# Two-layer diffusion backbone on one core: out projection of the last layer by token tiles in sequence, three modulation groups moved a layer ahead, first up tiles in two halves of the tokens

## The chip, the cores and the metric

The kernel runs on one core of one Trainium2 chip. The metric is device microseconds (us) from start to end of the program; lower is better. Engines are called PE (matmul; PEld is its weight load), DVE (vector), ACT (scalar), POOL (GpSimd) and SP (whose queue issues most DMAs).

## The reference

Two post-norm layers over 256 latent and 256 context tokens, width 1024. What the change touches:

```python
for i in range(DEPTH):                                   # DEPTH = 2
    need_ctx = i < DEPTH - 1                             # the last layer needs the latent tokens alone
    mod = (s_lat @ ada_w[i] + ada_b[i])[:, None, :]      # 1024 -> 6 * 1024
    sh1, sc1, g1, sh2, sc2, g2 = jnp.split(mod, 6, -1)
    u = modulate(h, sh1, sc1)                            # layer_norm(h) * (1 + sc1) + sh1
    ...                                                  # u @ w_in, then four token mixers
    mix = merge_branches((y_hy, y_sw, y_rw, y_df), p_gt, w_branch[i], w_out[i])   # ends with acc @ w_o
    h = layer_norm(DN_ALPHA * h + g1 * mix, ln1_g[i], ln1_b[i])
    f = conv_ffn(modulate(h, sh2, sc2), ffn_w_up[i], ffn_conv_w[i], ffn_conv_b[i], ffn_w_down[i])
    h = layer_norm(DN_ALPHA * h + g2 * f, ln2_g[i], ln2_b[i])
    ...                                                  # the same for the context tokens if need_ctx
```

## The kernel before

The 512 tokens are four tiles of 128: 0 and 1 context, 2 and 3 latent. Layer 0 works on all four, layer 1 (the last) on tiles 2 and 3 after its mixers have used the context; there `N.t0` is 256, the first token that counts. Every weight comes from HBM as a tile `w` of 128x1024 numbers (512 KB, by SP's queue, three buffers), is cast by ACT to `whi` (L197) and its remainder is taken by DVE or POOL as `wlo` (L201). Activations are split in the same way (`uh`/`ul`, `ah`/`al`), and every product is three matmuls: hi by hi, hi by lo, lo by hi. All matmuls of `mm` stand in one line (L174), all transposes in another (L178).

The work is written as Python generators that are woven by hand. `weave` runs a dense generator (matmuls of a projection) and, for a share of its cost, pulls steps from `N.work` (norms and the like). `col_tile` makes one 128-column tile of a projection: weight, then 24 matmuls over 8 values of k. It also pulls `N.rate` steps of the side generator `N.side`. The Tile framework's scheduler then orders each engine's instructions once more, so what stands next to what is only seen in the built program.

**Modulation.** `ada(l, groups)` makes the six modulation vectors of layer l in 12 groups. A group is 5 steps: four weight chunks (DMA `w<-in_adaw`, 512 KB each; matmuls `bkd<-w,sst`), then an ACT copy `adas`, four transposes `bkd<-cstt,adas` and a DVE reduction `mod`. Before, layer 1's groups 0 to 3 run beside the up tiles of layer 0's FFN, 4 to 9 beside the column tiles of layer 1's mixers (what is left over runs after the last of them, `N.weave(N.side, 0.0)`), and 10 and 11 after layer 1's out projection. `gate_out` and `gate_in` send a finished gate vector through HBM, to be broadcast.

**Out projection of the last layer** (`out_proj`, tiles 2 and 3, 8 weights k of `wout`, 96 matmuls of 512 columns). With `skew` 5, both tiles take k = 0 to 2; then tile 2 takes k = 3 to 7 while the weights are kept (three of them in tiles of their own, `wh`/`wl`), and tile 3 takes them after. The banks of tile 2 and the first half of tile 3 are called `bkd`, the last one `bko`. `finish` multiplies the banks by the gate and adds the residual, with sums. `hooks` issues the row vectors `lg`, `lb` and then loads and splits the first four weights of the FFN's up projection ahead (`pw`, to `ph`/`pl`).

**Tail.** For each tile: `sum_stats` (ACT square, POOL power), `post_norm` (two DVE operations), `sum_stats` again, `norm` to `xn` (one POOL operation of 1024 columns), `modulate` (8 transposes; for each k an ACT operation to `uh`, POOL to `u`, DVE to `ul`). Then the up tiles: 44 column tiles of 256 tokens.

Of the kernel before, what the change touches and what calls it, by code (L numbers as in the profile page):

```python
# [10 lines left out]
AF = mybir.ActivationFunctionType  # L11
ALU = mybir.AluOpType
# [100 lines left out]
class Feed:  # L113


    def __init__(self, net, items):
        self.net, self.items, self.loaded, self.ready = net, list(items), [], []
        self.cutting = iter(())
# [37 lines left out]
class Net:  # L156
    def __init__(self, ctx, tc, a, out):
        self.ctx, self.tc, self.nc, self.a, self.out = ctx, tc, tc.nc, a, out
        self.work, self.pre, self.pool_cols = [], [], 0
        self.side, self.rate = iter(()), 0  # L160
        self.lo = self.nc.vector
        self.aside, self.done, self.feed = [], set(), None
        self.ps = ctx.enter_context(tc.tile_pool(name="ps", bufs=1, space=PSUM))
        self.cp = ctx.enter_context(tc.tile_pool(name="cp", bufs=1))
        self.wp = ctx.enter_context(tc.tile_pool(name="wp", bufs=1))
        self.up = ctx.enter_context(tc.tile_pool(name="up", bufs=1))
# [76 lines left out]
    def dense(self, ps, hi, lo, c0, xh, xl, nk, t0, t1):  # L243

        for k in range(nk):
# [8 lines left out]
                self.feed.step()  # L254
            yield 3 * 0.216 * (t1 - t0) / 512

    def col_tile(self, src, part):

        hi, lo = self.wsplit(src)
        for _ in range(self.rate):  # L260
            next(self.side, None)
        ps = self.bank("d")[:, 0:part[1] - part[0]]
        yield from self.dense(ps, hi, lo, lambda k: k * 128, self.uh, self.ul, 8, *part)
        return ps
# [181 lines left out]
    def norm(self, src, dst, stats, pool=None):  # L446

        nc = self.nc
        m, rs = stats
        if pool is None:  # L450
            nc.vector.tensor_scalar(dst, src, m, rs, op0=ALU.subtract, op1=ALU.mult)
            return
        nm = pool.tile([128, 1], F32, tag="lnns", name="lnns", bufs=2)
        nc.vector.tensor_scalar(nm, m, rs, -1.0, op0=ALU.mult, op1=ALU.mult)
        nc.gpsimd.tensor_scalar(dst, src, rs, nm, op0=ALU.mult, op1=ALU.add)

    def u_tiles(self):
# [1174 lines left out]
    def out_proj(self, l, pool, src, nk, lhs, tiles, h, gate, tail, skew, hooks, folded):  # L1632

        nc = self.nc
        hooks = iter(hooks)

        def weight(k, last):
            w = self.wload(src(k))  # L1640
            if last and folded:
                g = gate[tiles[-2] // 2]
                c = 512
                nc.gpsimd.tensor_tensor(w[:, 0:c], w[:, 0:c], g[:, 0:c], ALU.mult)  # L1644
                nc.vector.tensor_tensor(w[:, c:1024], w[:, c:1024], g[:, c:1024], ALU.mult)
            x = k - nk + skew
            hl = None
            if last and 0 <= x < skew - 2:
                hl = [pool.tile([128, 1024], F32R, name=f"w{y}{x}") for y in "hl"]
            return next(self.wcut(w, 1, hl))  # L1650

        def step(w, i, k, halves=(0, 1)):
            (whi, wlo), (ah, al), ts = w, lhs(k), slice(i * 128 - self.t0, i * 128 + 128 - self.t0)
            for hf in halves:
                cs = slice(hf * 512, hf * 512 + 512)
                self.mm(ps[i, hf], ah[:, ts], whi[:, cs], k == 0, False)
                self.mm(ps[i, hf], ah[:, ts], wlo[:, cs], False, False)
                self.mm(ps[i, hf], al[:, ts], whi[:, cs], False, k == nk - 1)

        def finish(i):  # L1660
            sums = []
            for hf in range(2):
                sl = slice(hf * 512, hf * 512 + 512)
                if not folded:
                    nc.vector.tensor_tensor(ps[i, hf], ps[i, hf], gate[i // 2][:, sl], ALU.mult)
                sm = pool.tile([128, 1], F32, tag=f"lns{hf}", name="lns", bufs=2)
                nc.vector.scalar_tensor_tensor(h[i][:, sl], h[i][:, sl], ALPHA, ps[i, hf], ALU.mult, ALU.add, accum_out=sm)
                sums.append(sm)
            return sums
        pre = []  # L1670
        for p0 in range(0, len(tiles), 2):
            pr = tiles[p0:p0 + 2]
            last = p0 == len(tiles) - 2
            sk = skew if last else 0
            ps = {(i, hf): self.bank("m" if not last else "o" if i % 2 and hf else "d") for i in pr for hf in range(2)}
            ws = []
            for k in range(nk):
                w = pre.pop(0) if pre else weight(k, last)
                next(hooks, None)
                if k < nk - sk:  # L1680
                    for i in pr:
                        step(w, i, k)
                    yield 2.6
                else:
                    ws.append(w)
                    step(w, pr[0], k)
                    yield 1.3
            if not last:
                pre = [weight(k, p0 == len(tiles) - 4) for k in range(2)]
                self.pool_cols = 320  # L1690
            if not last:
                self.work.append(tail([(i, finish(i)) for i in pr]))
                continue
            self.work.append(tail([(pr[0], finish(pr[0]))]))
            for hf in range(2):
                for x in range(sk):
                    step(ws[x], pr[1], nk - sk + x, [hf])
                    yield 0.65
            self.work.append(tail([(pr[1], finish(pr[1]))]))
        for _ in hooks:  # L1700
            pass
# [38 lines left out]
def backbone(ctx, tc, a, out):  # L1740
    N = Net(ctx, tc, a, out)
    nc = tc.nc
# [4 lines left out]
    for l in range(DEPTH):  # L1747
        need_ctx = l == 0
# [1 line left out]
        streams = (0, 1) if need_ctx else (1,)  # L1750
        N.t0 = 0 if need_ctx else 256
        n = 512 - N.t0
        N.side = N.ada(l, range(4 if l else 4, 10))
        ox = ExitStack()
        if 1:
            with ExitStack() as mx:
# [110 lines left out]
                with ExitStack() as ax:  # L1867
# [5 lines left out]
                    N.weave(N.swa_cols(l, ap_, need_ctx, xs), 0.0)  # L1873
                    N.weave(N.side, 0.0)
                    N.gate_out(l, 16, 0.5)
                    N.rate = 0
                    dp_ = ax.enter_context(tc.tile_pool(name="dp", bufs=1))
                    N.feed = Feed(N, [(a["win"][l, T_DF + t], None) for t in DF_ORDER]
# [46 lines left out]
        op = ox.enter_context(tc.tile_pool(name="op", bufs=1, side="right"))  # L1925
        lg, lb = (op.tile([128, 1024], F32, name=x) for x in ("lg", "lb"))
        N.u_tiles()
        kc, npre = (3, 4) if need_ctx else (0, 4)
        fx, fwx = ExitStack(), ExitStack()
        if kc:  # L1930
            fp1 = fx.enter_context(tc.tile_pool(name="fp1", bufs=1))
# [2 lines left out]
        def hooks():  # L1934
            yield
            G = [lambda t=t, x=x: nc.sync.dma_start(t, a[x][l].partition_broadcast(128))
                 for t, x in ((lg, "ln1_g"), (lb, "ln1_b"))]
            W = [lambda x=x: N.ahead(fw, a["wup"][l, x]) for x in range(npre)]
            for f in W + G if l == 0 else G + W:
                f()  # L1940
                yield

        def tail(its):
            xs = []
            for i, sums in its:
# [6 lines left out]
            yield from N.modulate(op, l, 1, xs, its[0][0])  # L1952
        N.pool_cols = 0 if need_ctx else 0
        N.weave(N.out_proj(l, op, lambda k: a["wout"][l, k], 8, lambda k: ahl[k], tiles, N.h, g1, tail,
                           (2 if need_ctx else 5), hooks(), l == 1 and 0), 0.4)
        hid = []

        def more2(k, part):
# [3 lines left out]
        if kc:  # L1962
            N.pre = (N.pre + [None] * (2 * kc - npre)) * 2
            N.side, N.rate = N.ada(0, (10, 11)), 2
            with tc.tile_pool(name="fu", bufs=1) as fu:
                N.weave(N.ffn_up(l, fu, [(k, CTX) for k in range(kc)], 256, hid, fp1, more2), 0.5)
                N.weave(N.side, 0.0)
                N.gate_out(l, 40, 1.0)
                N.flush()
                N.pool_cols = 0  # L1970
                ox.close()
                N.weave(N.ffn_up(l, fu, [(k, LAT) for k in range(kc)], 256, hid, fp1, more2), 0.0)
            fwx.close()
        else:
            N.weave(N.ada(l, (10, 11)), 0.0)
            N.gate_out(l, 40, 1.0)
            N.flush()
            N.pool_cols = 0
            ox.close()
        if 1:  # L1980
            fp2 = fx.enter_context(tc.tile_pool(name="fp2", bufs=1))
            with tc.tile_pool(name="fu", bufs=1) as fu:
                fdx = ExitStack()
                fd = fdx.enter_context(tc.tile_pool(name="fd", bufs=1, side="right"))
                g2 = {s: fd.tile([128, 1024], F32, name=f"g2{s}") for s in streams}
                lg, lb = N.row_vec(fd, "ln2_g", l, "lg"), N.row_vec(fd, "ln2_b", l, "lb")
                if l == 0:
                    N.side = N.ada(1, range(4))
                N.weave(N.ffn_up(l, fu, [(k, (N.t0, 512)) for k in range(kc, NKD)], n, hid, fp2,
                                 more2), 0.1)  # L1990
                N.weave(N.side, 0.0)
                N.rate = 0
                N.flush()
# [107 lines left out]
```

## Time and profile before

| | |
|---|---|
| three runs | 1866.68, 1867.2, 1871.5 us; median 1867.2 us |
| profiled execution | 1865.73 us, of which the span from the first to the last instruction is 1863.7 us |
| mean granted clock of TensorE | 0.967 |
| busy share of the span | PE 91%, PEld 72%, DVE 62%, ACT 42%, POOL 34% |
| chain that ended last | PE 60%, DVE 15%, ACT 5%, POOL 3%, DMA 3% |
| DMA | 241.37 MB, mean 130 GB/s |

PE is busy nine tenths of the span, but not evenly: for long stretches every microsecond is full, and in a few (the end of the last layer's out projection is one) it waits for norms. A matmul that is added costs its whole time in the first kind, and nothing in the second.

### The profile page before, as it was taken

Reading aid. Unit: us, or ns where it says so; the run is one execution under the profiler, and the core shown is the slowest. Engines: PE = TensorE matmul, PEld = TensorE weight load, DVE = VectorE, ACT = ScalarE, POOL = GpSimd, SP = SyncE. Lnnn points to the kernel's source line nnn. Section 1 sums busy time; section 2 is a strip of 40 time slices with the busy share of each in tenths; the row PEclk is TensorE's granted clock in tenths of the full one; section 3 lists DMA queues with packets and bytes.
Section 4 is the critical chain, followed back from the end, with each engine's and each line's share of the span. In section 5 each row is a group of like instructions: output and inputs, shape, how many; then the busy total and the mean of one; then the engine's idle time right before and its main releaser. Section 6 shows DMA issues by size and latency. Waiting matters only on the chain.

```text
span 1863.7 us, 36355 instructions
## 1 busy us (share of the span) xinstructions
PE 1704.9 (91%) x14618; PEld 1347.3 (72%) x14618; DVE 1146.3 (62%) x2204; ACT 783.1 (42%) x1571; POOL 639.7 (34%) x782
## 2 busy tenths in 40 slices
PE   6999999998999988999999998899888988879986
PEld 2566777876777766867788866677677887679965
DVE  5566455765665477544555557573766665658787
ACT  2323344653332445433344444344553344456632
POOL 2313143543544126110110065243455664131153
PEclk9999999998999999999999999999999999889999
DMA  7353312211111455344334556654123222645543
GB/s 303 126 201 107 130 57 63 77 60 53 45 56 52 140 190 180 126 147 147 124 102 133 184 170 200 216 170 142 51 85 93 93 69 80 235 143 186 186 142 113
DMA packets 73456, 241.37 MB, mean 130 GB/s; under 512 B 8518, under 2 KB 17096, under 8 KB 73032
## 3 DMA queue, kind: packets, MB, share of 16 engines
q1 hardware_dynamic: 69336, 229.80, 37.7%
q10 hardware_dynamic: 3952, 9.25, 1.6%
q8 instruction: 115, 1.88, 0.4%
q14 instruction: 53, 0.43, 0.1%
HBM read 235.84 MB, written 2.13 MB: 128 GB/s over the span
## 4 chain that ended last, share of the span: by engine, by line
PE 60%; DVE 15%; ACT 5%; POOL 3%; DMA 3%; issue 3%; POOLq 0%; SPq 0%; ACTq 0%; DVEq 0%
PE bkd L174 45%; PE bkm L174 8%; PE bkm L1361 2%; PE bko L174 2%; DVE wlo L201 2%; PE bkm L178 2%; DMA w<-in_wdn 1%; ACT whi L197 1%; DVE sV L1339 1%; DVE dmx L977 1%; ACT dp L980 1%; POOL wlo L201 1%; DMA w<-in_wout 1%; DVE dp L996 1%; DVE ul L478 1%
## 5 line engine op out<-in xcount | busy, mean ns | idle before, releaser
L174 PE MATMUL bkd<-uh,whi 128*128 128x256 f32 (+1 forms) x1624 | 584.7, 360 | 6.9 <-ACT whi L197 3.2
L174 PE MATMUL bkd<-uh,wlo 128*128 128x256 f32 (+1 forms) x1624 | 552.5, 340 | 3.9 <-DVE wlo L201 3.5
L174 PE MATMUL bkd<-ul,whi 128*128 128x256 f32 (+1 forms) x1624 | 550.7, 339 | 0.0
L197 ACT CAST whi<-w 128x256 fp32r<-128x256 f32 (+1 forms) x532 | 333.7, 661 | 271.1 <-PE bkd L174 117.5
L201 DVE TENSOR_TENSOR wlo<-w,whi 128x1024 fp32r<-128x1024 f32 (+3 forms) x247 | 282.9, 1150 | 196.5 <-ACT whi L197 195.5
L201 POOL TENSOR_TENSOR wlo<-w,whi 128x256 fp32r<-128x256 f32 (+2 forms) x328 | 274.4, 856 | 320.5 <-ACT whi L197 316.6
L174 PEld LDWEIGHTS bkd<-uh,whi 128*128 128x128 f32 x1624 | 310.1, 191 | 85.4 <-ACT whi L197 23.8
L174 PEld LDWEIGHTS bkd<-uh,wlo 128*128 128x128 f32 x1624 | 310.0, 191 | 41.3 <-DVE wlo L201 4.1
L174 PEld LDWEIGHTS bkd<-ul,whi 128*128 128x128 f32 x1624 | 310.9, 191 | 26.2 <-issue 0.7
L1721 POOL TENSOR_TENSOR fc<-fc,fc 128x256 f32<-128x256 f32 (+1 forms) x47 | 46.1, 980 | 331.5 <-DVE fc L329 312.1
L174 PE MATMUL bkd<-w,sst 128*32 128x512 f32 x348 | 82.1, 651 | 17.4 <-DMA w<-in_adaw 17.4
L1583 POOL TENSOR_TENSOR acc<-acc,tg 128x512 f32<-128x512 f32 (+1 forms) x32 | 32.5, 1017 | 142.8 <-DVE tg L1582 129.7
L324 ACT ACTIVATE fc<-bkd,vec 128x256 f32<-128x256 f32 (+1 forms) x94 | 60.7, 646 | 7.5 <-PE bkd L174 7.5
L327 DVE SCALAR_TENSOR_TENSOR fc<-bkd,vec,fc 128x255 f32<-128x255 f32 (+1 forms) x94 | 54.8, 583 | 11.6 <-ACT fc L324 11.6
L174 PE MATMUL bkd<-wlo,hh 128*128 128x512 f32 x126 | 52.4, 416 | 9.7 <-DVE wlo L201 7.0
L237 ACT CAST hh<-fc 128x256 fp32r<-128x256 f32 (+1 forms) x47 | 23.2, 493 | 84.9 <-POOL fc L1721 84.9
L329 DVE SCALAR_TENSOR_TENSOR fc<-bkd,vec,fc 128x255 f32<-128x255 f32 (+1 forms) x94 | 55.3, 589 | 2.9
L238 DVE TENSOR_TENSOR hl<-fc,hh 128x256 fp32r<-128x256 f32 (+1 forms) x47 | 25.6, 545 | 47.3 <-ACT hh L237 47.3
L238 DVE TENSOR_TENSOR wbl<-wb,wbh 128x256 fp32r<-128x256 f32 x48 | 30.7, 639 | 37.0 <-ACT wbh L237 36.6
L174 PE MATMUL bkd<-y,wbh 128*128 128x512 f32 (+1 forms) x192 | 53.4, 363 | 0.0
L174 PE MATMUL bkd<-whi,hh 128*128 128x512 f32 x126 | 48.5, 399 | 3.7 <-DVE fc L329 2.4
L1644 POOL TENSOR_TENSOR w<-w,g 128x512 f32<-128x512 f32 x22 | 38.3, 1745 | 34.9 <-DMA w<-in_wdn 30.9
(473 smaller groups left out, 2983.5 us busy)
## 6 DMA issues: line engine op xcount, KB each, us to landing
w<-in_adaw SPq DMA_DIRECT2D x87, 512.0 KB, 4.0
w<-in_wup SPq DMA_DIRECT2D x82, 512.0 KB, 3.5
w<-in_wdn SPq DMA_DIRECT2D x66, 512.0 KB, 3.5
w<-in_wg SPq DMA_DIRECT2D x64, 512.0 KB, 3.6
w<-in_win SPq DMA_DIRECT2D x58, 512.0 KB, 3.6
w<-in_wout SPq DMA_DIRECT2D x24, 512.0 KB, 3.5
wb<-in_wbr SPq DMA_DIRECT2D x48, 128.0 KB, 3.4
pw<-in_wup SPq DMA_DIRECT2D x8, 512.0 KB, 4.4
```

Source lines behind the costliest of these rows:

```text
L174: self.nc.tensor.matmul(out, lhsT, rhs, start=start, stop=stop)
L178: self.nc.tensor.transpose(out, in_, self.ident[0:n, 0:n])
L197: self.nc.scalar.copy(hi[:, c], w[:, c])
L201: e.tensor_tensor(lo[:, c], w[:, c], hi[:, c].bitcast(F32), ALU.subtract)
L238: nc.vector.tensor_tensor(lo, src, hi.bitcast(F32), ALU.subtract)
L324: nc.scalar.activation(dst, ps, AF.Identity, bias=b, scale=w1)
L327: nc.vector.scalar_tensor_tensor(d3[:, :, 1:256], p3[:, :, 0:255], w0, d3[:, :, 1:256], ALU.mult, ALU.add)
L329: nc.vector.scalar_tensor_tensor(d3[:, :, 0:255], p3[:, :, 1:256], w2, d3[:, :, 0:255], ALU.mult, ALU.add)
L1361: nc.tensor.matmul(ps[r, o:o + 32], L(r, d, c, x, e, j), R[r, d, 2 * e + j, :], start=True, stop=True, tile_position=(r.start, r.start))
L1583: nc.gpsimd.tensor_tensor(acc, acc, tg[:, 0:n], ALU.add)
L1644: nc.gpsimd.tensor_tensor(w[:, 0:c], w[:, 0:c], g[:, 0:c], ALU.mult)
L1721: nc.gpsimd.tensor_tensor(ab[0], ab[0], ab[1], ALU.mult)
```

## The change

1. Layer 1's groups 4, 5 and 6 move from its mixers into layer 0's FFN (7 groups there instead of 4); groups 10 and 11 move from the tail into the mixers, which so run 5 groups instead of 6. The second gate of layer 1 is sent right after the first.
2. The out projection of the last layer takes all k for tile 2, then all k for tile 3 (`skew` 8; six weights kept in tiles of their own). Five empty hooks stand ahead of the loads of the up weights, which are three instead of four.
3. The tail of tile 2 is written out first; then `up_first` multiplies the first three up weights by tile 2's 128 tokens alone; then comes the tail of tile 3, and `col_tile` takes the other 128 tokens of those three tiles.
4. Where `t0` is set, `norm` writes half of `xn` on ACT and half on DVE, instead of all of it on POOL. This also meets one norm of layer 0's last tile, which runs in layer 1.

```diff
+    def up_first(self, l, n):
+        for _ in range(n):
+            hi, lo = self.pre.pop(0)
+            ps = self.bank("d")
+            yield from self.dense(ps[:, 0:128], hi, lo, lambda k: k * 128, self.uh, self.ul, 8, 256, 384)
+            self.begun.append((hi, lo, ps))
     def col_tile(self, src, part):
+        if self.begun:
+            hi, lo, ps = self.begun.pop(0)
+            yield from self.dense(ps[:, 128:256], hi, lo, lambda k: k * 128, self.uh, self.ul, 8, 384, 512)
+            return ps[:, 0:256]
...
+        if self.t0:
+            nc.scalar.activation(dst[:, 0:512], src[:, 0:512], AF.Identity, scale=rs, bias=nm)
+            nc.vector.tensor_scalar(dst[:, 512:1024], src[:, 512:1024], rs, nm, op0=ALU.mult, op1=ALU.add)
+            return
         nc.gpsimd.tensor_scalar(dst, src, rs, nm, op0=ALU.mult, op1=ALU.add)
...
                     step(ws[x], pr[1], nk - sk + x, [hf])
+                    next(hooks, None)
...
-        N.side = N.ada(l, range(4 if l else 4, 10))
+        N.side = N.ada(l, range(7, 12) if l else range(4, 10))
...
                     N.gate_out(l, 16, 0.5)
+                    if l:
+                        N.gate_out(l, 40, 1.0)
...
-        kc, npre = (3, 4) if need_ctx else (0, 4)
+        kc, npre = (3, 4) if need_ctx else (0, 3)
...
-            for f in W + G if l == 0 else G + W:
+            for f in W + G if l == 0 else G + [lambda: None] * 5 + W:
...
-                           (2 if need_ctx else 5), hooks(), l == 1 and 0), 0.4)
+                           (2 if need_ctx else 8), hooks(), l == 1 and 0), 0.4)
...
-            N.weave(N.ada(l, (10, 11)), 0.0)
-            N.gate_out(l, 40, 1.0)
+            while len(N.work) > 1:
+                for _ in N.work.pop(0):
+                    pass
+            N.weave(N.up_first(l, npre), 0.0)
             N.flush()
...
-                    N.side = N.ada(1, range(4))
+                    N.side = N.ada(1, range(7))
```

**PE at the end of the last layer's out projection.** Before, in PE's order (`bko<-whi` are the last matmuls of the out projection, `w,sst` and `adas` the modulation, `cstt,xn` a tile's transposes, `ph` a weight loaded ahead):

```order
L174 MATMUL bko<-whi,al_16886 128x512
L174 MATMUL bkd<-w,sst 32x512 x8
L178 MATMUL bkd<-cstt,adas 128x128 x4
L174 MATMUL bkd<-w,sst 32x512 x4
L178 MATMUL bkm<-cstt,xn 128x128 x8
L174 MATMUL bkd<-w,sst 32x512 x4
L178 MATMUL bkd<-cstt,adas 128x128 x4
L178 MATMUL bkm<-cstt,gt 16x128
L178 MATMUL bkm<-cstt,xn 128x128 x8
L174 MATMUL bkd<-uh_16994,ph_17079 128x256
L174 MATMUL bkd<-uh_16994,ph_17097 128x256
L174 MATMUL bkd<-uh_16994,ph_17115 128x256
```

After, the modulation is gone from there, and tile 2's transposes are followed at once by the up tiles at half width:

```order
L174 MATMUL bko<-whi,al_16947 128x512
L178 MATMUL bkm<-cstt,xn 128x128 x8
L174 MATMUL bkd<-uh_17055,ph_17185 128x128
L174 MATMUL bkd<-uh_17055,ph_17266 128x128
L174 MATMUL bkd<-uh_17055,ph_17275 128x128
L174 MATMUL bkd<-ul_17063,ph_17185 128x128
```

Further on in the same order, tile 3's transposes stand behind the last of the 72 half-width matmuls, and 72 more follow them:

```order
L174 MATMUL bkd<-ul_17070,ph_17275 128x128
L174 MATMUL bkd<-uh_17062,pl_17276 128x128
L178 MATMUL bkm<-cstt,xn 128x128 x8
L174 MATMUL bkd<-uh_17055,ph_17185 128x128
L174 MATMUL bkd<-uh_17055,ph_17266 128x128
```

What moved: eight transposes of tile 3 can no longer be reached before all first halves are done.

**DVE in the tail after the change** (`ul` are tile 2's, the last row tile 3's; L466 and L469 are the norm's scale and its DVE half of `xn`, here of tile 3, whose residual is `h_6900`):

```order
L494 SCALAR_TENSOR_TENSOR ul_17069<-bkm,sc1p,u_17255 128x128
L494 SCALAR_TENSOR_TENSOR ul_17070<-bkm,sc1p,u_17259 128x128
L454 TENSOR_SCALAR lnve<-lnve 128x1
L466 TENSOR_SCALAR lnns<-lnm,lnrs 128x1
L469 TENSOR_SCALAR xn<-h_6900,lnrs,lnns 128x512
L494 SCALAR_TENSOR_TENSOR ul_17063<-bkm,sc1p,u_17441 128x128
```

So tile 3's second statistics are finished on DVE only behind all eight `ul` of tile 2; before, the norm stood on POOL.

**ACT at the same place.** Before, from the last weight of the out projection to the squares of the two tiles (`h_6899` is tile 2's residual):

```order
L197 CAST whi<-w 128x1024
L440 ACTIVATE xn,lnve<-h_6899,lnnm 128x1024
L382 COPY adas<-bkd 128x512
L440 ACTIVATE xn,lnve<-h_6899,lnnm 128x1024
L440 ACTIVATE xn,lnve<-h_6900,lnnm 128x1024
```

After, the third cast of the first row below is that of the fourth up weight, whose buffer is that of the out projection's weight k = 6:

```order
L197 CAST whi<-w 128x1024 x3
L452 ACTIVATE xn,lnve<-h_6899,lnnm 128x1024
L197 CAST whi<-w 128x1024
L452 ACTIVATE xn,lnve<-h_6899,lnnm 128x1024
L452 ACTIVATE xn,lnve<-h_6900,lnnm 128x1024
L468 ACTIVATE xn<-h_6899,lnns,lnrs 128x512
```

Tile 2's first square moved behind a cast that needs a buffer which the out projection still reads.

## Rows read from the trace of the kernel before

**Rows 1.** Windows: us, busy us of PE, PEld, DVE, ACT, POOL, clock, DMA share, GB/s.

```profile
900.00:920.00 20.00, 20.00 (x89) 14.60 (x88) 9.60 (x14) 7.53 (x10) 2.59 (x2) 1.00 0.45 151
...
1620.00:1630.00 10.00, 6.51 (x31) 1.72 (x30) 6.50 (x24) 2.37 (x4) 1.47 (x1) 0.75 0.57 208
1630.00:1640.00 10.00, 5.42 (x28) 2.20 (x20) 4.74 (x11) 5.10 (x13) 5.47 (x10) 0.57 0.42 126
1640.00:1650.00 10.00, 4.46 (x18) 3.72 (x19) 5.84 (x18) 6.19 (x14) 5.42 (x11) 0.60 0.57 193
```

**Rows 2.** Timeline of ACT, layer 0's FFN: start, us, line, operation (idle before, releaser).

```profile
904.66 0.78 ACT L324 ACTIVATE fc<-bkd,vec 128x512 f32<-128x512 f32 x1
...
918.04 0.78 ACT L324 ACTIVATE fc<-bkd,vec 128x512 f32<-128x512 f32 x1
...
923.99 0.77 ACT L324 ACTIVATE fc<-bkd,vec 128x512 f32<-128x512 f32 x1
...
929.76 0.77 ACT L324 ACTIVATE fc<-bkd,vec 128x512 f32<-128x512 f32 x1
...
1000.90 0.77 ACT L324 ACTIVATE fc<-bkd,vec 128x512 f32<-128x512 f32 x1
```

**Rows 3.** Timeline of PE, end of layer 1's mixer columns.

```profile
1275.97 1.91 PE L174 MATMUL bkd<-w,sst 128*32 128x512 f32 x12
...
1281.11 0.50 PE L174 MATMUL bkd<-uh,whi 128*128 128x512 f32 x1 [1.83 <-ACT whi L197]
```

**Rows 4.** Chain of waits at three places: start, us, what.

```profile
1155.73 1.20 POOL h L455
...
1277.06 3.57 DMA w<-in_win
...
1621.72 3.58 DMA w<-in_adaw
```

**Rows 5.** Timeline of PE, out projection of the last layer.

```profile
1597.16 0.63 PE L174 MATMUL bkd<-whi,al 128*128 128x512 f32 x1
...
1599.72 0.63 PE L174 MATMUL bkd<-wlo,ah 128*128 128x512 f32 x1
...
1620.31 0.40 PE L174 MATMUL bko<-whi,al 128*128 128x512 f32 x1
```

**Rows 6.** Timeline of all engines, tail of the last layer's out projection.

```profile
1618.16 1.30 DVE L1665 TENSOR_TENSOR bkd<-bkd,g 128x512 f32<-128x512 f32 x2 [1.29 <-PE bkd L174]
...
1629.11 0.19 DVE L388 TENSOR_REDUCE mod<-bkd 128x8 f32<-128x32 f32 x1 [2.71 <-PE bkd L178]
...
1631.95 2.24 POOL L455 TENSOR_SCALAR xn<-h,lnrs,lnns 128x1024 f32<-128x1024 f32 x1 [0.43 <-ACT xn L440]
...
1643.85 2.02 POOL L455 TENSOR_SCALAR xn<-h,lnrs,lnns 128x1024 f32<-128x1024 f32 x1 [0.43 <-ACT gr L407]
...
1647.29 2.90 ACT L475 ACTIVATE uh<-bkm,mod,sc1p 128x128 fp32r<-128x128 f32 x8 [3.61 <-PE bkm L178]
...
1648.25 2.80 DVE L478 SCALAR_TENSOR_TENSOR ul<-bkm,sc1p,u 128x128 fp32r<-128x128 f32 x8 [3.45 <-POOL u L476]
...
1649.03 0.41 PE L174 MATMUL bkd<-uh,pl 128*128 128x256 f32 x1
...
1652.02 0.41 PE L174 MATMUL bkd<-ul,ph 128*128 128x256 f32 x1
...
1652.39 0.28 PE L174 MATMUL bkd<-uh,ph 128*128 128x256 f32 x1
...
1653.83 0.28 PE L174 MATMUL bkd<-ul,ph 128*128 128x256 f32 x1
```

**Rows 7.** Timeline of PE and its weight loads in layer 1's mixers.

```profile
1288.51 0.33 PE L174 MATMUL bkm<-msk,idr 128*128 128x128 f32 x1
1288.62 0.19 PEld L174 LDWEIGHTS bkd<-uh,whi 128*128 128x128 f32 x1
...
1288.73 0.19 PEld L174 LDWEIGHTS bkd<-ul,whi 128*128 128x128 f32 x1
```

More of the change, by code (lines that the diff above doesn't have):

```diff
@@ L161, in __init__ @@
         self.lo = self.nc.vector
-        self.aside, self.done, self.feed = [], set(), None
+        self.aside, self.done, self.feed, self.begun = [], set(), None, []
         self.ps = ctx.enter_context(tc.tile_pool(name="ps", bufs=1, space=PSUM))
```

## Prediction

> **What bounds the kernel now.** I read the page first: PE is busy 91% of the span, so the windows come next, since a mean over stages tells little. In layer 0's FFN 20.00 of 20 us are full at clock 1.00 [rows 1]; there PE alone sets the end, and a matmul that is added costs its full time. At the end of the last layer's out projection PE has 6.51, 5.42 and 4.46 busy us in three windows of 10, at clocks 0.75, 0.57 and 0.60 [rows 1]: it waits for norms, and what it does then it does in part at the lower of its two levels. The chain of waits and the timeline show what it waits for. Behind the last matmul, 1620.31, stands a load of modulation weights of 3.58 us [rows 4, 5]; DVE sits idle for 2.71 us until a modulation reduction can run at 1629.11, and the norms' small operations are queued behind that; POOL writes `xn` of tile 2 in 2.24 us from 1631.95 and that of tile 3 in 2.02 from 1643.85 [rows 6]. So the change takes work off a place where PE waits, and puts some of it where PE is full.
>
> **The change part by part.**
>
> *Three groups into layer 0's FFN.* One up tile there is one `fc` operation of ACT (L324), and its pitch is PE's. Without modulation it is (1000.90 - 929.76) / 13 = 5.47 us. With one chunk per tile it is (918.04 - 904.66) / 2 = 6.69, so a chunk costs 1.22; with the four transposes (918.04 to 923.99) it is 5.95, so these cost 0.48 [rows 2]. A group is 4 x 1.22 + 0.48 = 5.35 us, three are +16.0. The 15 more steps find room beside the up tiles (36 column tiles, 35 steps). What could hide them is idle PE, and there is none [rows 1]. The 12 more loads of 512 KB stand in SP's queue among those of the up weights; the same pattern is in the four groups that run there already, and their pitch holds its price. Bounds: 14.6 (the chunk alone, four times, without the transposes) to 17.
>
> *One group fewer in the mixers of layer 1.* All 12 groups need 5 steps each: 30 become 25, and the last five go. Before, after the last column tile PE runs chunks for 1.91 us at 1275.97; the differential-attention columns behind them start at 1281.11, since their weight's load (3.57 us from 1277.06) stood in SP's queue behind four modulation loads [rows 3, 4]. Without those, the weight is loaded ahead. I let the columns start behind the gate and value transposes at about 1276.4: -4.7. Bounds: 3.0 (the chunks alone, 1.9 and half as much for one chunk a tile earlier) and 6.0 (1281.11 less the end of the column tile before). The second gate, now sent there, adds one small transpose and a DMA behind which SP has loads in stock.
>
> *The norm on ACT and DVE.* In layer 1 it also meets one norm of layer 0's last tile: POOL's 1.20 us, with PE waiting [rows 4]; halves on two engines take about half of it: -0.5, at least 0, at most 1.
>
> *Out projection.* Tile 2's banks were done when DVE's gate started at 1618.16, 2.15 us before the last matmul began [rows 5, 6]. In sequence tile 2 has 48 of 96 matmuls in program order, which would be some 11 us before the end; but in PE's order the scheduler fills with tile 3 whatever waits for a weight, and tile 2's last matmul is number 78 of 96. The first three weights can no longer start early, beside the end of the branches: in that stretch PE ran a 512-column matmul per (1599.72 - 1597.16) / 6 = 0.43 us [rows 5], against 5.47 / 24 = 0.23 at full clock [rows 2]. Laying the 96 out with a start at about 1597.6, 10.5 of them at 0.43 and the rest at 0.23, puts tile 2's end at about 1617.9 (nothing gained) and the end of all at about 1622, 1.4 later than before. That counts in the tail, where it is late for tile 3.
>
> *The tail.* Tile 2's `xn` was whole at 1634.2 (1631.95 + 2.24). The wait of 2.71 is gone, and about 1.6 of POOL's 2.24; both together would give 1629.9. Against it, tile 2's first square now stands on ACT behind a cast that needs the buffer of the out projection's k = 6, and DVE has a weight's remainder between. I take the middle, 1632. Transposes, then `uh` and `ul` of a tile from 1647.29 to 1648.25 + 2.80 = 1651.05, 3.76 us [rows 6], so PE starts the first halves at about 1633.7.
>
> What a 128-column matmul costs has no row of its own in a stream. The 256-column ones take (1652.02 - 1649.03) / 14 = 0.213 at the low clock and (1653.83 - 1652.39) / 12 = 0.12 at the full one [rows 6]; half of the columns would be 0.06 as a lower end. But each has its own weight load, and loads that stand close follow at 1288.73 - 1288.62 = 0.11, while one 128-column matmul lasts 0.33 [rows 7]. I take 0.12, the same as at 256: a matmul cut in two is then paid twice. As the upper end I take the low clock throughout, 0.213.
>
> The Trainium skill (TensorE: Matmul & The Clock Gate, "Back-to-back issue gap") gives a sustained spacing of 81 ns at 128 columns and 131 ns at 512. The row at 512 columns is 0.23, which does not agree; by the page's 81 ns the 96 halves at full clock would take 7.8 us instead of 11.5, and the sum below would be 3.7 lower.
>
> So: 24 at 0.213 (PE has waited before) to 1638.8, 48 at 0.12 to 1644.6. Tile 3's norm is ready before that, at about 1640: its last statistics stand on DVE behind tile 2's eight `ul`, which end near 1636.9. But its transposes stand behind all 72 halves on PE, so they start at 1644.6; 0.8 for eight, 3.76 for `uh` and `ul` with the first 24 halves inside, 48 at 0.12: 1655. Before, three up tiles' worth of 24 were done at 1652.39 + 51 x 0.12 = 1658.5 (1652.39 is number 21 of them). Gain 3.5 to 4; I take 4, since the fourth up weight is now split early. Bounds: 10.6 gained (0.06 for a half, its 48 in 2.9 twice) and 6.4 lost (0.213 throughout: 72 x 0.213 = 15.3 to 1649, transposes at 2.0, `uh` and `ul`, 48 x 0.213 = 10.2, to 1665).
>
> **Sum:** 16.0 - 4.7 - 0.5 - 4.0 = +6.8. The profiled execution took 1865.7, so 1872.5 there; the median of the runs shown is 1.5 above it, 1867.2, so I predict 1874.0. A difference under 0.3% (5.6 us) is about what a measurement of this kernel can't tell from no change.
>
> **The rivals.**
>
> *Cheap halves.* A matmul of 128 columns costs by its columns, 0.06. The tail then gains 10.6: +0.2, 1867.4, no change to be told. For it: the columns are half. Against it: the loads at 0.11 [rows 7]. The page's spacing lies between this and my forecast.
>
> *Dear halves.* The clock stays low through the first halves and the second, as in the 20 us before 1650 [rows 1]: the tail loses 6.4, +17.2, 1884. For it: PE is fed by `uh` and `ul` at one k per half a us and so has gaps. Against it: in before the clock rose within 5 us of a stream that began the same way.
>
> *Faster.* The wait for the modulation reduction was all that held the norms of both tiles, and without it tile 3's `xn` follows the out projection as closely as DVE's operations allow. To come out 5.6 faster, the tail must gain 16.0 - 4.7 - 0.5 + 5.6 = 16.4 us instead of 4: the second halves must end by 1642, so tile 3's transposes must start near 1632, with all first halves done. For it: PE waits some 14 of 30 us there [rows 1]. Against it: the order, in which tile 3's statistics stand behind tile 2's `ul`. At a gain of 16.4 the time is 1861.6.
>
> *The sequence changes nothing.* The scheduler mixes the tiles as before; this is in my sum already (tile 2 at number 78). Were tile 2 done 5 us earlier than I think, the tail would gain up to 3.8 more, since PE holds tile 3 (1644.6) and its norm is ready only at 1640: +3.0, 1870.
>
> **How the numbers follow.** Forecast (gain of the tail 1 to 8, so +3 to +10) 0.55, of which 0.40 are slower by over 0.3% and 0.15 within; cheap halves 0.15, all within; an early tile 2 0.08, 0.05 within and 0.03 slower; dear halves 0.12, slower; faster 0.10. Together slower 0.55, same 0.35, faster 0.10. The range runs from 1865 (the cheap halves with a mixer gain at its bound of 6) to 1881 (half way from the forecast to the dear halves); beyond it I leave about 0.08 below and 0.1 above. The forecast's own range is 1870 to 1877.
>
> **What would show it.** In layer 0's FFN 12 more chunks at a pitch of 6.7 instead of 5.47, and everything behind about 16 us later; the columns of differential attention 4 to 5 us closer to the column tile ahead of them; first halves from near 1634 on the old axis, 0.11 to 0.12 apart at full clock, tile 3's transposes right behind the 72nd with `xn` waiting for PE. The prediction is wrong if the chunks cost clearly less than 1.2, if halves come at 0.06 to 0.08, or if tile 3's transposes wait for its norm and not for PE.

## The result and the profile after

The changed kernel takes 1888.95 us (median of 4 runs, 1886.12 to 1896.44), the kernel before in the same series 1869.35: the ratio is 1.0116, 95% interval 1.0093 to 1.0140, so about 20 us slower. Slower was forecast, 1874.0; the time lies outside the range of 1865 to 1881. Of the rivals the one called dear halves, 1884, is the nearest. Three single executions that stand far apart from all others (2338 to 4059 us) are left out of the ratios and intervals below.

The profiled execution took 1889.6 us, 24 more than that of before. The windows of the changed kernel: the one in the FFN is that of [rows 1], and the tail lies some 14 us later on this axis than there:

```profile
900.00:920.00 20.00, 20.00 (x89) 14.60 (x88) 9.58 (x14) 7.53 (x10) 2.59 (x2) 1.00 0.46 154
...
1640.00:1650.00 10.00, 3.80 (x16) 3.30 (x16) 7.61 (x22) 5.73 (x12) 4.39 (x8) 0.50 0.26 84
1650.00:1660.00 10.00, 10.00 (x49) 10.00 (x48) 2.31 (x7) 2.42 (x5) 1.56 (x4) 0.50 0.00 0
1660.00:1670.00 10.00, 9.97 (x46) 9.47 (x46) 2.81 (x8) 2.94 (x8) 2.83 (x8) 0.50 0.01 1
1670.00:1680.00 10.00, 10.00 (x48) 10.00 (x49) 2.26 (x5) 3.23 (x5) 0.73 (x1) 0.50 0.43 158
1680.00:1700.00 20.00, 20.00 (x158) 20.00 (x158) 12.37 (x20) 10.60 (x17) 1.54 (x3) 0.91 0.32 108
```

The reader is to see two things that a busy share hides. PE is full from 1650 to 1680 (on the axis of before from 1636, where it still waited until 1648), but with some 48 matmuls in 10 us, at a clock of 0.50, the lower of its two levels. From 1680, with 256-column matmuls, it does 158 in 20.

The timeline of the changed kernel in that place, which answers to [rows 6]:

```profile
1631.49 1.30 DVE L1681 TENSOR_TENSOR bkd<-bkd,g 128x512 f32<-128x512 f32 x2 [1.86 <-PE bkd L174]
...
1644.84 0.81 ACT L468 ACTIVATE xn<-h,lnns,lnrs 128x512 f32<-128x512 f32 x1
...
1645.70 1.97 PE L178 MATMUL bkm<-cstt,xn 128*128 128x128 f32 x8 [9.57 <-ACT xn L468]
...
1649.26 0.41 PE L174 MATMUL bkd<-uh,pl 128*128 128x128 f32 x1
...
1652.77 0.81 ACT L468 ACTIVATE xn<-h,lnns,lnrs 128x512 f32<-128x512 f32 x1 [1.16 <-DVE lnns L466]
...
1663.55 0.41 PE L174 MATMUL bkd<-uh,pl 128*128 128x128 f32 x1
1663.76 1.93 PE L178 MATMUL bkm<-cstt,xn 128*128 128x128 f32 x8
...
1681.10 0.41 PE L174 MATMUL bkd<-uh,pl 128*128 128x128 f32 x1
1681.32 0.52 PE L174 MATMUL bkd<-uh,whi 128*128 128x256 f32 x1
...
1683.13 0.41 PE L174 MATMUL bkd<-uh,wlo 128*128 128x256 f32 x1
...
1683.63 0.28 PE L174 MATMUL bkd<-uh,wlo 128*128 128x256 f32 x1
```

But for the first four behind each tile's transposes, which come a little slower, every half lasts 0.41 and they follow at 0.213, from 1649.26 to the last at 1681.10; at 256 columns the duration falls to 0.28 after 2.2 us. Tile 3's `xn` is whole at 1653.58, and its transposes start at 1663.76: they wait 10 us for PE, behind tile 2's halves.

The FFN of layer 0, ACT's rows that answer to [rows 2]. The three added groups show as a pitch of 6.69 (930.99 to 951.06 is three up tiles) where it was 5.47:

```profile
924.30 0.78 ACT L336 ACTIVATE fc<-bkd,vec 128x512 f32<-128x512 f32 x1
930.99 0.77 ACT L336 ACTIVATE fc<-bkd,vec 128x512 f32<-128x512 f32 x1
...
951.06 0.78 ACT L336 ACTIVATE fc<-bkd,vec 128x512 f32<-128x512 f32 x1
...
1016.44 0.78 ACT L336 ACTIVATE fc<-bkd,vec 128x512 f32<-128x512 f32 x1
```

The same up tile as 1000.90 of before comes at 1016.44. Layer 1's differential-attention columns, which began at 1281.11 [rows 3], begin at 1292.39, with a wait of 1.10 instead of 1.83:

```profile
1292.39 0.50 PE L174 MATMUL bkd<-uh,whi 128*128 128x512 f32 x1 [1.10 <-ACT whi L197]
```

Cut at the same instructions, the two profiled executions differ like this (us; each stretch from the timeline's starts):

| stretch | before | after | difference |
|---|---|---|---|
| start to the residual sums that end layer 0 | 1131.1 | 1146.7 | +15.6 |
| to layer 1's first key rotation (`sxk`) | 133.6 | 132.0 | -1.6 |
| to the first scores of the windowed attention | 23.0 | 20.5 | -2.5 |
| to the end of the mixers (last `ovr`) | 289.6 | 292.4 | +2.8 |
| to the last matmul of the out projection | 42.9 | 44.0 | +1.1 |
| to the end | 243.4 | 252.2 | +8.8 |

### The profile page after: what moved, and what is told of

Its sections match the earlier page's. It is cut to its first block, busy times and chain, and to the rows that moved or that the text cites. A ratio compares the mean times of both kernels' runs of the same rounds, so it can differ in the third digit from the quotient of the medians.

```text
span 1887.9 us, 36504 instructions
## 1 busy us (share of the span) xinstructions
PE 1729.1 (92%) x14690; PEld 1370.4 (73%) x14690; DVE 1143.3 (61%) x2207; ACT 787.0 (42%) x1574; POOL 636.0 (34%) x779
## 5 line engine op out<-in xcount | busy, mean ns | idle before, releaser
L201 DVE TENSOR_TENSOR wlo<-w,whi 128x1024 fp32r<-128x1024 f32 (+3 forms) x245 | 277.3, 1137 | 205.6 <-ACT whi L197 205.1
L174 PE MATMUL bkd<-whi,hl 128*128 128x512 f32 x126 | 50.2, 400 | 0.0
```

The source lines that it names most:

```text
L174: self.nc.tensor.matmul(out, lhsT, rhs, start=start, stop=stop)
L201: e.tensor_tensor(lo[:, c], w[:, c], hi[:, c].bitcast(F32), ALU.subtract)
```

## The experiments

Ratios are to the kernel before, run on the same chip in the same series. Single executions of the kernel before spread from 1857 to 1880 there, so ratios with their intervals carry the verdicts, and a stretch of one profile only where it is far outside that.

**Groups back (`g_back`).** The changed kernel, layer 0 with four groups as before, the mixers of layer 1 with eight:

```diff
-        N.side = N.ada(l, range(7, 12) if l else range(4, 10))
+        N.side = N.ada(l, range(4, 12) if l else range(4, 10))
...
-                    N.side = N.ada(1, range(7))
+                    N.side = N.ada(1, range(4))
```

> The changed kernel, but layer 0's FFN runs layer 1's groups 0 to 3 alone, as before, and layer 1's mixers run 4 to 11 (40 steps). Clock theory (16 us of the loss are the three groups on a full PE, the rest is the low clock under the half-width up tiles): layer 0's FFN is 15.5 us shorter, the mixers pay 9 to 15 for 15 more steps, so the time is 1875 to 1883 where the changed kernel has 1889; the clock in the first 30 us of up tiles stays at 0.50 as in the changed kernel. Rival (the groups cost little where they are, and the loss is all in the tail): within 3 us of 1889.

1894.52, ratio 1.0143 (1.0111 to 1.0174): no gain, by the medians some 5 more than the changed kernel, though the two intervals overlap; the time is outside both expectations. Layer 0 is back at 1131.1, but the stretch from `sxk` to the windowed attention's first scores is 41.8 us instead of 20.5. PE and SP's queue there:

```profile
1260.62 28.49 SPq L387 DMA_DIRECT2D w<-in_adaw  x12
```

```profile
1279.55 4.26 PE L174 MATMUL bkd<-w,sst 128*32 128x512 f32 x12 [1.57 <-DMA w<-in_adaw]
...
1284.65 1.05 PE L174 MATMUL bkd<-w,sst 128*32 128x512 f32 x4 [0.84 <-DMA w<-in_adaw]
```

The column tiles of the mixers carry about 25 steps; what is over runs in one piece behind them, at the pace of loads and copies (twelve loads in one run), with hardly any other work beside it. Three groups cost 21 us there and 15.6 beside layer 0's full PE. So the price of a group depends on what is beside it, and a stage in which PE has idle time is not cheaper if the group doesn't run inside that time.

**Full width (`full_up`).** The changed kernel without `up_first`; both tails, then the up tiles over 256 tokens:

```diff
-            N.weave(N.up_first(l, npre), 0.0)
```

> The changed kernel without the halves: both tails first, then all up tiles over 256 tokens. Clock theory: the first up tile starts only when tile 3's norm is done, some 9 us later than the first halves did, but 256-column matmuls bring the clock back within about 5 us of their start, so three up tiles' worth is done some 12 us earlier: 1874 to 1879 where the changed kernel has 1889. Rival (what holds the tail are the norms and the out projection in sequence, and the halves only fill a wait): 1886 to 1893.

1875.31, ratio 1.0032 (1.0013 to 1.0051): 13.6 us of the 20 are gone, as the clock theory had it. The first up tile starts 19.8 us behind the out projection's last matmul, where the first halves started 11.9 behind it; and yet three tiles are done 30.5 us behind that matmul instead of 45.6. PE's timeline:

```profile
1655.21 0.41 PE L174 MATMUL bkd<-uh,pl 128*128 128x256 f32 x1
...
1657.77 0.41 PE L174 MATMUL bkd<-uh,pl 128*128 128x256 f32 x1
...
1658.16 0.28 PE L174 MATMUL bkd<-ul,ph 128*128 128x256 f32 x1
```

They start at the same low clock, pass to the full one after 4 us, and run at 0.12 from there.

**Groups alone (`groups_only`).** The kernel before with part 1:

```diff
-        N.side = N.ada(l, range(4 if l else 4, 10))
+        N.side = N.ada(l, range(7, 12) if l else range(4, 10))
...
                     N.gate_out(l, 16, 0.5)
+                    if l:
+                        N.gate_out(l, 40, 1.0)
...
-            N.weave(N.ada(l, (10, 11)), 0.0)
-            N.gate_out(l, 40, 1.0)
...
-                    N.side = N.ada(1, range(4))
+                    N.side = N.ada(1, range(7))
```

> The kernel before with part 1 alone (7 groups in layer 0's FFN, 5 in the mixers, none in the tail). Clock theory: +15.5 in layer 0's FFN, -1 to -4 in the mixers, -3 to -6 in the tail, whose DVE no longer waits for the modulation: +6 to +12 over the kernel before, 1874 to 1881. Rival (the groups cost little): within 3 us of the kernel before.

1872.58, ratio 1.0016 (0.9998 to 1.0034): between the two, +2.7 with an interval from 0 to 6, so the +6 to +12 of the theory is too much, and "no cost" could not be excluded by this run. In the profile the FFN's price is there (layer 0's stretch 1143.9 against 1131.1), the way from `sxk` to the first scores is 22.1 us against 23.0, and from the out projection's last matmul to the end it is 239.7 instead of 243.4.

**Norms alone (`norm_only`).** The kernel before with part 4:

```diff
+        if self.t0:
+            nc.scalar.activation(dst[:, 0:512], src[:, 0:512], AF.Identity, scale=rs, bias=nm)
+            nc.vector.tensor_scalar(dst[:, 512:1024], src[:, 512:1024], rs, nm, op0=ALU.mult, op1=ALU.add)
+            return
```

> The kernel before with part 4 alone (xn by halves on ACT and DVE). Expected from the trace after, where the two halves end 0.85 us after the scale instead of 2.4: -1 to -1.5 at the layer boundary and -1.5 to -3 in the tail, so -2 to -4.5, 1863 to 1866. Rival (the halves wait behind other work on ACT and DVE and the gain is eaten): within 1.5 us of the kernel before.

1862.52, ratio 0.9961 (0.9938 to 0.9985): 7 us faster, somewhat more than expected; the interval (3 to 12) holds the -4.5. The halves of `xn` take 0.55 and 0.81 us side by side where POOL's operation took 2.24 [rows 6]:

```profile
1639.68 0.55 DVE L457 TENSOR_SCALAR xn<-h,lnrs,lnns 128x512 f32<-128x512 f32 x1
1639.74 0.81 ACT L456 ACTIVATE xn<-h,lnns,lnrs 128x512 f32<-128x512 f32 x1
```

**A filled wait (`warm_halves`).** The changed kernel with matmuls whose result nobody reads between the out projection and tile 2's transposes:

```diff
+            ps = N.bank("d")
+            for _ in range(40):
+                N.mm(ps, ahl[0][0][:, 0:128], N.pre[0][0][:, 0:512], True, True)
             while len(N.work) > 1:
```

> The changed kernel with 40 matmuls of 512 columns, whose result nobody reads, put on PE between the out projection and tile 2's transposes, where PE waits 9.6 us. Clock theory: the first halves then begin at the full clock and run at 0.11 to 0.12 instead of 0.213 for at least their first few us; if the clock then falls again under halves alone, the rest runs at 0.213 and the gain is 1 to 4 us, if it holds, both halves end 12 to 14 us earlier (1875). Rival (128 columns cost 0.213 whatever the clock): no gain, 1889.

1888.49, ratio 1.0107 (1.0074 to 1.0140), the same as the changed kernel and the rival's time; the 1 to 4 us that I expected did not come. PE's timeline, then the windows:

```profile
1635.13 9.49 PE L174 MATMUL bkd<-ph,ah 128*128 128x512 f32 x40
1644.87 1.10 PE L178 MATMUL bkm<-cstt,xn 128*128 128x128 f32 x8 [0.25 <-ACT xn L468]
...
1648.09 0.33 PE L174 MATMUL bkd<-ul,ph 128*128 128x128 f32 x1 [1.35 <-DVE ul L494]
1648.26 0.28 PE L174 MATMUL bkd<-uh,pl 128*128 128x128 f32 x1
1648.37 0.28 PE L174 MATMUL bkd<-uh,ph 128*128 128x128 f32 x1
...
1649.10 0.42 PE L174 MATMUL bkd<-uh,pl 128*128 128x128 f32 x1
```

```profile
1635.00:1645.00 10.00, 9.75 (x43) 7.54 (x42) 7.77 (x19) 5.96 (x9) 2.33 (x3) 1.00 0.35 105
1645.00:1650.00 5.00, 3.43 (x23) 3.05 (x23) 4.36 (x10) 3.02 (x8) 4.91 (x9) 0.88 0.00 0
1650.00:1660.00 10.00, 10.00 (x49) 10.00 (x48) 1.55 (x7) 2.06 (x3) 0.68 (x2) 0.50 0.00 0
1660.00:1670.00 10.00, 9.97 (x46) 9.47 (x46) 2.81 (x8) 2.94 (x8) 2.85 (x8) 0.50 0.14 36
1670.00:1680.00 10.00, 10.00 (x49) 10.00 (x49) 2.35 (x5) 3.23 (x5) 0.73 (x1) 0.50 0.30 123
```

At the full clock a half costs 0.11 (1648.26 to 1648.37), close to the 0.12 that I had taken; so the rival's reason, 0.213 whatever the clock, is wrong. But only some ten halves ran at that price: the clock falls at 1648.8, behind 1.35 us of waiting and a handful of halves, and does not come back in the 30 us up to 1680 that halves keep PE full. That rules out that the halves were slow only because PE had waited 9.57 us before them; what made the clock fall, the 1.35 us or the halves, this run leaves open.

**Norms and groups (`norm_groups`).** The kernel before with parts 1 and 4, the edits of the two runs above together.

> The kernel before with parts 1 and 4 (groups and norms), the out projection and the up tiles as before. If the two parts add (groups +2.7, norms -7.3 by the last runs): 4 to 5 below the kernel before. If part 2, the sequence, costs nothing, this must equal the kernel without halves, 5.5 above the kernel before; a gap between the two is the price of the sequence.

1873.58, ratio 1.0031 (1.0013 to 1.0050). It equals the kernel without halves (1.0032), so the sequence has no price that can be told. But by these runs the two parts do not add: +0.16% and -0.39% apart, +0.31% together. The first series had its single parts on one chip and the two together on another, so three kernels ran once more on one chip.

**The same three again (`groups_2`, `norm_2`, `norm_groups_2`).** Edits as above.

> Part 1 alone again, beside the two runs below on one chip, since parts 1 and 4 did not add (+0.16%, -0.39%, together +0.31%). If the gap was scatter of single executions: 1.001 to 1.005. If the groups really cost little without the norms: 1.000 to 1.002 again.

> Part 4 alone again. If the gap was scatter: 0.996 to 0.999. If the norms really give 7 us where the modulation is still in the tail: 0.995 to 0.997.

> Parts 1 and 4 again. If the parts add but for the 1 us that their profiles of the tail share: the sum of the two ratios above, within 0.1%. If they work against each other: 0.4% or more above that sum.

Ratios 1.0026 (1.0006 to 1.0047), 0.9979 (0.9956 to 1.0002) and 1.0010 (0.9987 to 1.0032): +0.26% and -0.21% give +0.05%, and +0.10% was measured: here the parts add, and the gap of 0.54% in the first series did not come back. Over both series the groups cost some 4 us, the norms give some 6, and both together cost some 4, which is still 5 or 6 above the sum, with an uncertainty about as large. One part of that is in the traces. From the out projection's last matmul to the first up tile it is 27.5 and 27.3 us in the two profiles of before, 23.8 and 23.8 with the groups, 23.0 and 21.3 with the norms, but 21.2 and 21.1 with both: of the same wait each part alone takes 3.6 and 4.4 to 6.1, and both together only 6.3. So 2 to 3.5 us can be gained once, not twice; the rest of the gap can't be told from scatter.

**Norms and sequence (`norm_seq`).** The changed kernel with groups and up tiles as before, so that parts 2 and 4 are left:

```diff
-        N.side = N.ada(l, range(7, 12) if l else range(4, 10))
+        N.side = N.ada(l, range(4, 10))
...
-                    if l:
-                        N.gate_out(l, 40, 1.0)
...
-            while len(N.work) > 1:
-                for _ in N.work.pop(0):
-                    pass
-            N.weave(N.up_first(l, npre), 0.0)
+            N.weave(N.ada(l, (10, 11)), 0.0)
+            N.gate_out(l, 40, 1.0)
...
-                    N.side = N.ada(1, range(7))
+                    N.side = N.ada(1, range(4))
```

> The kernel before with parts 2 and 4 (sequence and norms), groups and up tiles as before. By the trace of the changed kernel the sequence ends the out projection 1.1 us later and brings tile 2's norm no earlier: with norms alone at -7.3, this is 5 to 7 below the kernel before. Rival (the sequence itself costs 10, as the sum of the medians so far would have it): +2 to +4.

1860.41, ratio 0.9948 (0.9922 to 0.9975): the fastest version here, 5 to 15 us under the kernel before (5 to 7 was expected) and faster than the changed kernel by some 28. Against norms alone (0.9961 and 0.9979) the sequence makes no difference that the intervals can tell.

**Before again (`before_again`).** The kernel before, for a second profile.

> The kernel before, unchanged, for a second profile: how far do the stretches of one kernel differ between two executions. Expected: layer 0 up to its FFN's end and the last up tiles agree within 1.5 us, the mixers of layer 1 within 5, at clocks that differ by 0.01 to 0.02; ratio 1.000.

Ratio 1.0009 (0.9991 to 1.0027). Its profiled execution took 1872.0 us, 6.3 more than the one shown above. The windows of the mixers, first the kernel before, then this run:

```profile
1287.76:1577.40 289.64, 257.38 (x4408) 229.46 (x4407) 176.30 (x421) 133.11 (x373) 152.59 (x224) 0.95 0.26 79
```

```profile
1286.90:1581.30 294.40, 262.31 (x4407) 234.27 (x4406) 177.00 (x420) 133.18 (x373) 153.36 (x224) 0.93 0.25 76
```

The same work takes 4.8 us longer at a clock of 0.93 instead of 0.95; layer 0 took 1127.8 instead of 1131.1, 3.3 apart where I had expected at most 1.5. So the +2.8 of the mixers in the table above says nothing of the change. The traces of all fourteen runs, cut at the same instructions, show what of the table stands. Layer 0's stretch is 1127.8 to 1131.1 in the six with four groups in its FFN and 1143.9 to 1147.0 in the eight with seven. The stretch behind the out projection is 252.2 to 252.5 in the three whose halves ran at the low clock, and 232.8 to 243.4 in the others. These two differences are clear of the spread. The -1.6 up to `sxk` and the +1.1 of the out projection are not: with and without the part in question these stretches lie between 131.9 and 135.7 and between 42.8 and 46.0.

**Padded halves (`pad_halves`).** The changed kernel with each half streamed twice, so that a matmul has 256 columns; the second copy lands in columns that are overwritten or never read:

```diff
             xs, ls = xh[k][:, t0:t1], xl[k][:, t0:t1]
+            if t1 - t0 == 128:
+                xs, ls = (x.unsqueeze(1).to_broadcast([128, 2, 128]) for x in (xs, ls))
...
-            yield from self.dense(ps[:, 0:128], hi, lo, ...
+            yield from self.dense(ps[:, 0:256].rearrange("p (a b) -> p a b", a=2), hi, lo, ...
...
-            yield from self.dense(ps[:, 128:256], hi, lo, ...
+            yield from self.dense(ps[:, 128:384].rearrange("p (a b) -> p a b", a=2), hi, lo, ...
```

> The changed kernel with every half-width matmul doubled to 256 columns: the 128 tokens are streamed twice, the second copy into columns of the bank that are overwritten or never read. Nothing else changes; PE has twice the columns to stream, with as many matmuls and weight loads. Clock theory (the clock stays at its lower level under halves, and at that level 128 columns cost the 0.213 that 256 cost): the first 20 or so still take 0.213, then the clock rises and the rest take 0.12; 144 halves take 10 to 13 us less, so 1875 to 1879 where the changed kernel has 1889. Rival (128 columns are cheaper than 256, or the clock stays low for what PE did before them): the same 1889, or up to 8 more.

1875.34, ratio 1.0033 (1.0010 to 1.0055): twice the columns, 13.6 us less. The windows of this run:

```profile
1650.00:1655.00 5.00, 4.60 (x20) 4.31 (x21) 4.03 (x14) 3.55 (x9) 3.90 (x9) 0.50 0.00 0
1655.00:1660.00 5.00, 5.00 (x43) 5.00 (x43) 0.56 (x2) 0.82 (x1) 0.00 (x0) 0.97 0.00 0
1660.00:1665.00 5.00, 4.47 (x36) 4.02 (x35) 1.78 (x6) 2.83 (x8) 2.19 (x7) 1.00 0.00 0
1665.00:1670.00 5.00, 5.00 (x44) 5.00 (x43) 1.52 (x4) 1.24 (x3) 0.65 (x2) 1.00 0.58 177
```

The padded halves start as slow as the others (20 matmuls in 5 us at 0.50), then the clock rises and it is 43 in 5 us, with as many instructions and weight loads as the changed kernel has. It stays up through the wait for tile 3. From the out projection's last matmul to the first full tile it is 33.9 us instead of 45.6. So these 13.6 us are the clock that does not rise under the halves, and nothing in the norms, the loads or the order, which this run has as the changed kernel has them. What is left, 0.33%, is what the kernels without halves have too: 0.32% at full width, 0.31 and 0.10% with norms and groups alone.

## Why the prediction was wrong, point by point

- **What a half costs, and at which clock: this step failed.** I wrote "24 at 0.213 (PE has waited before) to 1638.8, 48 at 0.12 to 1644.6", and let the second halves run at 0.12 too. The 0.12 is right for a half at the full clock (0.11 in the run with the filled wait). But I let the clock rise as it had in before under 256-column matmuls, and it did not: it stayed at 0.50 and the 144 halves took 0.213, to the last. By the prediction's own chain, with 0.213 throughout, the tail loses 6.4, with three tiles done at 1665 on before's axis; they were done at 1667.0, since all 72 second halves are paid behind tile 3's transposes (15.7 us, 1665.60 to 1681.32) where I had let 24 hide beside `uh` and `ul`. Out projection and tail together lost 9.9 (1.1 + 8.8) where 4.0 gained was forecast. The case was there as dear halves with 12 in 100, priced at 1884, and was left out of the range, above which I left only 0.1. My argument against it was a stream of another width.
- **The price of the groups was right.** 16.0 was forecast for layer 0's FFN; the same up tile is 15.5 later, and the stretch 15.6 longer in this pair of profiles.
- **One group fewer in the mixers was mis-sized.** -4.7 was forecast, and -2.5 to the first scores came (over the profiles the stretch is 20.5 to 22.3 with five groups and 23.0 to 25.0 with six): the columns still wait 1.10 us for their weight, and a second gate transpose waits 1.6 us ahead of them. What lies behind that in the mixers is within the spread of one kernel.
- **The norm at the layer boundary** was forecast at -0.5, with at most 1; the stretch is 1.6 shorter in one pair of profiles, which is within the spread, so no run shows a gain there. Norms alone gave 4 to 7 us in two series, most of it in the tail (240.1 and 237.1 in its two profiles, 243.4 and 242.8 in those of before), where I had counted 1.6 for tile 2 alone.
- **The out projection**: 1.1 later came where 1.4 was forecast, but two profiles of before alone differ by 3 there, so this is not shown either way. The sequence has no price that can be told, by `norm_groups` and `norm_seq`.
- **Tile 2's norm and tile 3's** were right: on before's axis (14.3 less, by the table) `xn` of tile 2 is ready at 1631.4 (1632 forecast), the first half starts at 1633.3 (1633.7), tile 3's `xn` is ready at 1639.3 (1640) and waits for PE behind the 72nd half. So the halves did start 14 us earlier than up tiles had; at 0.213 that is worth less than nothing.
- **The rivals.** Cheap halves fell (0.11 at best). The faster one fell: tile 3's norm follows as the order said. An early tile 2 fell: its gate starts at 1631.49, which is 1617.2 on before's axis, where 1617.9 was forecast. The Trainium skill's 81 ns at 128 columns (TensorE: Matmul & The Clock Gate, "Back-to-back issue gap") was not seen at either level: 0.11 us at the full one, 0.213 at the lower. The Trainium skill's section "LDWEIGHTS (loading the stationary operand)" on that page gives the time of a weight load as columns / 1.2 in ns, by estimate 107 ns for 128. The 0.11 between halves at full clock agrees with that; the 0.213 at the lower level does not.

The sum of the steps, as this pair of profiles has them without the mixers' +2.8: 15.6 - 1.6 - 2.5 + 1.1 + 8.8 = +21.4, and +19.6 was measured between the medians. Of the 14.6 between this sum and the forecast's +6.8, 13.9 are the tail.

## What to carry to other kernels

A stream of 128-column matmuls kept PE full here and was still not granted the full clock; before cutting a matmul to fill a wait, look in the trace for a stream of that width and read its clock, and keep the cut only if it is paid at the low level too. Where such a stream can't be avoided, wider columns, even repeated ones, may be free: here 256 columns cost at the low level what 128 cost. And price work that is moved by what stands beside it at its new place: three modulation groups cost 15.6 beside a full PE, 21 where they ran alone at the end of a stage.

## What the runs showed of the hardware that I had not expected

- With PE busy 29.97 of 30 us on 128-column matmuls the granted clock stayed at 0.50 throughout (1650 to 1680 of the changed kernel), and rose 2.2 us after the first 256-column matmul; with the same matmuls padded to 256 columns it rose to 1.00 some 4 us into the stream.
- At the lower level 128 and 256 columns cost the same, 0.213 us each; at the full one 0.11 (`warm_halves`) and 0.12.
- Two executions of one kernel differ by 4.8 us in the mixers alone, at clocks of 0.93 and 0.95, so a single pair of profiles says little of a stretch that long.
